# Samples' selected branch: both selections, the prompt's output norms and the half-sequence tiles moved

## The chip, the cores and the metric

The kernel runs on one core of one Trainium2 chip. The metric is the device time of one execution in microseconds (us), lower is better. Engines are named as the profile names them: PE is TensorE's matmul (PEld its weight load), DVE VectorE, ACT ScalarE, POOL GpSimd, SP SyncE, which issues most DMAs. POOL issues the gathers from the paged caches.

## What is computed

One inference step of a decoder layer for a prompt (512 tokens) and eight sample sequences (4 new tokens each on 2048 cached ones). The part that matters is the sparse attention, for prompt and samples, and what follows it:

```python
h = rmsnorm(x, w['g_mix'])
(q, kc_new, vc_new, ks_new, vs_new, kw_new, vw_new, g_nsa, xm, vm, om, i_pre, f_pre) = split_cols(h @ w['w_in'])
...
k_cmp = compress(kc_all, *w['cmp_k'])      # 16-token strides through a 2-layer net
v_cmp = compress(vc_all, *w['cmp_v'])
# nsa_attend, per block of queries:
s_c = jnp.einsum('bkgqd,bkcd->bkgqc', qi, kc) - slopes * d_c
p_c = masked_softmax(s_c, d_c >= 0)
o_c = jnp.einsum('bkgqc,bkcd->bkgqd', p_c, vc)          # compressed branch
imp = cmp_to_sel(p_c.sum(2))
...
_, idx = lax.top_k(imp, n_top)                          # selection of 64-token blocks
s_s = jnp.einsum('bkgqd,bkqsd->bkgqs', qi, k_sel) - slopes * d_s
p_s = masked_softmax(s_s, d_s >= 0)
o_s = jnp.einsum('bkgqs,bkqsd->bkgqd', p_s, v_sel)      # selected branch
...                                                     # o_w: sliding window branch
o_nsa = rmsnorm(o_nsa, w['g_head_nsa']).reshape(b, t, NSA_W)
...
mix = jnp.concatenate([o_nsa, hm.reshape(b, t, MLSTM_W).astype(x.dtype)], axis=-1) @ w['w_out']
x = x + mix
```

Cross attention, a SwiGLU layer and a final norm follow.

## The kernel before, in words

The program is written as Python generators that are woven together (`weave`, `burst`, `paced`); a scheduler then sets the order of instructions on each engine by priorities, and each engine executes its own queue in that order. Tiles come from pools with a number of buffers, so an instruction that writes a tile waits until the buffer's readers are done.

The compression of the cached values, `compress(1)`, keeps PE full with products of the split weights (`bd<-w1h,xh` and its kind, L218 to L220). A high product is made of three: the operands are split into a high and a low part by `split` (L213 on ACT makes the high part, L214 on DVE or POOL the low one). Into the compression is woven `sample()`, the samples' sparse attention. It works on two groups `g` of four sequences each. For either group its window branch comes first, then:

- the *selection*: scores against the compressed keys (`quad` with `kcT`), a softmax (tile `pcs`, Exp at L1607), block sums, a product with `GS` (L1627) and the top blocks (`t8`, `mk`), from which POOL makes the mask `M4` (L1642);
- the *key part*: keys come in half-sequence tiles `gat` (128 x 1024, 512 KB) that POOL gathers (L573). A *key turn* transposes four 128x128 blocks on PE (`four_t`, L1517) into one of two PSUM banks `tp`; `evac` copies the bank to one of four tiles `kt`, three times on ACT (L206) for one on DVE (L208). Four key turns feed one *score product* `quad` (L1527, bank `sp`), whose masked minimum DVE takes (L1653). A group has 16 key turns and 4 score products;
- the *probabilities* (`SS`, five Exps at L1674 and L1672) and the *value part*: turns of `SS` into `PTs` and 64 value products (L1693) with value tiles, which use the same `gat` buffers.

After the first group's value part stands `finals_p`, the prompt's output norm: for four pairs of heads a product with the compressed values (L1398), its addition to `oF` (L1401) and its square (ACT, L1402), a product with a matrix of ones `bones` (L1407) that leaves the mean square in a bank, then x^(-1/2) as Ln (L1408) and Exp (L1413) on ACT, and the scaling of `oF` on DVE (L1414).

Once `oF` is scaled, `early_mix` splits it (`mh`, `ml`), and the output projection's first half of tokens (272 of 544) begins: 24 products `xa/bd/xc<-mh,whi` and kin for each 128 output columns. The weights `w_out` come in four chunks of 256 columns, each of two 128x1024 pieces. The first two are fetched early (one of them into the tile `cgat`), each later one by SP (L1830, L1832) when the chunk before it in the buffer `wraw` has been split (`whi` on ACT, `wlo` on DVE). In this stretch PE uses the first two chunks, 96 products; the products of the third and fourth follow the value part of the second group.

Of the kernel before, what the change touches and what calls it, by code (L numbers as in the profile page):

```python
# [21 lines left out]
BIG = 1e30  # L22
# [14 lines left out]
def body(tc, I, O, stage=99, dbg=None):  # L37
    nc = tc.nc
    with ExitStack() as top:
# [704 lines left out]
        def need(x):  # L744
            while x not in done:
                yield 1
# [644 lines left out]
        def finals_p(var):  # L1391
            yield from need(("p", 1))
            var = var[:, :2048].rearrange("p (a b n) -> p a b n", a=2, b=2)
            for j in range(5):
# [22 lines left out]
        def sample():  # L1417
# [85 lines left out]
            def load_win(nm, b):  # L1503
                t_ = sc.tile([128, 2, 4, 128], F32, name="gat", bufs=8)
# [32 lines left out]

            win = {(0, "k"): kwin(0), (0, "v"): vwin(0), (1, "k"): kwin(1)}
            yield 2
            for g in range(2):  # L1540
                bs = [4 * g + q for q in range(4)]
# [52 lines left out]
            kg = half("cache_k_slc", 0, 0)  # L1594
            for g in range(2):
# [6 lines left out]
                quad(pc[:, 0:127], bs, lambda q: kcT[:, bs[q], 0:127])  # L1602
                pcs = sc.tile([128, 128], F32, name="pcs")
                nc.vector.memset(pcs[:, 127:128], 0.0)
                nc.vector.tensor_tensor_reduce(pcs[:, 0:127], pc[:, 0:127], K0, 1.0, BIG, op0=OP.add, op1=OP.min,
                                               accum_out=nmn[:, 0:1])
                nc.scalar.activation(pcs[:, 0:127], pcs[:, 0:127], AF.Exp, scale=-1.0, bias=nmn[:, 0:1],  # L1607
                                     accum_out=rs[:, 0:1])
                nc.vector.reciprocal(rs[:, 3:4], rs[:, 0:1])
                nc.vector.tensor_scalar(pcs[:, 0:127], pcs[:, 0:127], rs[:, 3:4], None, op0=OP.mult)  # L1610
                blk = sc.tile([128, 32], F32, name="blk")
                edge = sc.tile([128, 32], F32, name="edge")
                p4 = pcs.rearrange("p (j r) -> p j r", r=4)
                nc.vector.tensor_reduce(blk, p4[:, :, 0:3], axis=AX.X, op=OP.add)
                nc.vector.tensor_copy(edge, p4[:, :, 3])
                nc.vector.tensor_tensor(edge[:, 1:32], edge[:, 1:32], p4[:, 0:31, 3], op=OP.add)
                nc.vector.scalar_tensor_tensor(blk, edge, 0.5, blk, op0=OP.mult, op1=OP.add)
# [5 lines left out]
                p = bank(ptp)  # L1623
                nc.tensor.transpose(p[:127, :128], pcs[:, 0:127], ident)
                nc.vector.tensor_copy(pct[:127, g], p[:127, :128])
                p = bank(ptp)
                nc.tensor.matmul(p[:, :32], GSf, blk, start=True, stop=True)  # L1627
                imp = sc.tile([128, 32], F32, name="imp")
                nc.vector.tensor_copy(imp, p[:, :32])
                ia = imp[:, 1:31]  # L1630
                t8 = sc.tile([128, 16], F32, name="t8")
                nc.vector.max(out=t8[:, 0:8], in_=ia)
# [953 lines left out]
```

## Time and profile before

| what | value |
| --- | --- |
| median of 3 runs | 1249.11 us (1246.6, 1249.11, 1251.46) |
| profiled execution | 1244.16 us, of which the span is 1242.4 us |
| granted TensorE clock, mean | 0.972 |
| PE busy | 1174.2 us, 95% of the span |
| DVE, ACT, POOL busy | 67%, 50%, 45% |
| DMA | 154.30 MB, mean 124 GB/s |

The profile is of one execution, on the slowest of its cores; here there is one. Around the span lie 1.8 us of the execution's time. Busy shares are means over stages with different limits, so the stretch from 440 to 612 us, where the change works, has to be read by itself.

### The profile page before, as it was taken

The numbers are of one execution on the slowest core, as the hardware profiler recorded it, in microseconds if no ns is written. First come the engines' busy times: TensorE is split into PE (matmuls) and PEld (weight loads), VectorE is DVE, ScalarE is ACT, GpSimd is POOL, SyncE is SP. The second block draws the span as 40 slices with busy tenths as digits, with TensorE's granted clock in tenths as the row PEclk, the third lists the DMA queues.
The fourth block names the chain that finished last, engine by engine and source line by source line (L and its number), as shares of the span: only waits on it lengthen the run. The fifth ranks groups of instructions, "written<-read, shape, count | busy, mean of one in ns | idle before, by whom it ended". The sixth has DMA issues, their size and how long they took to land.

```text
span 1242.4 us, 24591 instructions
## 1 busy us (share of the span) xinstructions
PE 1174.2 (95%) x9220; PEld 1066.4 (86%) x9220; DVE 830.3 (67%) x1901; ACT 615.7 (50%) x1418; POOL 564.0 (45%) x686
## 2 busy tenths in 40 slices
PE   7999999899997989988899998999999999999996
PEld 5998999588885879846699977599899999999996
DVE  6336683567887787544566575544987887878874
ACT  5235665745646434474543233433575565565452
POOL 1013353566766366442243100034796586486442
PEclk9998999989997989998899999999999999999998
DMA  7324240141253184585468399650023322322411
GB/s 232 102 53 104 86 152 1 53 135 43 74 175 115 57 294 152 176 276 154 122 168 179 111 221 278 233 169 2 1 100 105 103 94 96 118 94 77 137 52 73
DMA packets 141769, 154.30 MB, mean 124 GB/s; under 512 B 17449, under 2 KB 123689, under 8 KB 141394
## 3 DMA queue, kind: packets, MB, share of 16 engines
q1 hardware_dynamic: 131922, 119.17, 32.1%
q0 software_dynamic: 9728, 33.56, 8.3%
q8 instruction: 73, 1.20, 0.4%
q14 instruction: 46, 0.38, 0.1%
HBM read 141.67 MB, written 13.12 MB: 125 GB/s over the span
## 4 chain that ended last, share of the span: by engine, by line
PE 53%; DVE 7%; DMA 5%; ACT 2%; issue 1%; POOL 1%; SPq 1%; POOLq 0%; DVEq 0%; ACTq 0%
PE xc L2260 7%; PE xa L2260 7%; PE bd L2260 6%; PE tp L2260 5%; PE bd L218 3%; PE bd L220 3%; PE bd L219 3%; PE xa L1296 2%; DMA wraw<-in_w_out 2%; DMA mkv<-in_cache_mem_k 2%; PE tp L1517 1%; PE bd L2159 1%; PE xc L218 1%; PE xc L219 1%; PE xc L220 1%
## 5 line engine op out<-in xcount | busy, mean ns | idle before, releaser
L214 POOL TENSOR_TENSOR al<-fraw,ah 128x512 fp32r<-128x512 f32 (+1 forms) x104 | 127.1, 1224 | 146.8 <-ACT ah L213 118.9
L213 ACT ACTIVATE whi<-wraw 128x1024 fp32r<-128x1024 f32 (+3 forms) x74 | 63.0, 890 | 70.1 <-DMA wraw<-in_w_xv 28.4
L214 DVE TENSOR_TENSOR wlo<-wraw,whi 128x1024 fp32r<-128x1024 f32 (+3 forms) x74 | 75.0, 1041 | 31.2 <-ACT whi L213 31.0
L213 ACT ACTIVATE ah<-fraw 128x512 fp32r<-128x512 f32 (+1 forms) x112 | 66.0, 594 | 43.8 <-PE xc L2260 11.8
L218 PE MATMUL bd<-w1h,xh 128*128 128x256 f32 x256 | 82.9, 326 | 0.0
L1198 POOL TENSOR_TENSOR xs<-xf 128x256 f32<-128x256 f32 x64 | 57.3, 902 | 48.5 <-PE xa L1296 29.7
L220 PE MATMUL bd<-w1h,xl 128*128 128x256 f32 x256 | 75.7, 298 | 1.4 <-DVE xl L214 1.4
L219 PE MATMUL bd<-w1l,xh 128*128 128x256 f32 x256 | 76.1, 298 | 0.0
L1296 PE MATMUL xa<-ws,xs 128*128 128x256 f32 x256 | 70.9, 399 | 1.9 <-DVE bq L1469 1.0
L625 POOL TENSOR_SCALAR sb<-sb,rs,gat 128x128 f32<-128x128 f32 (+3 forms) x64 | 46.2, 726 | 56.0 <-DVE rs L624 41.9
L213 ACT ACTIVATE xh<-xf 128x512 fp32r<-128x512 f32 x64 | 40.1, 632 | 43.6 <-DVE xf L1191 19.8
L213 ACT ACTIVATE ah<-sp 128x512 fp32r<-128x512 f32 (+1 forms) x64 | 35.6, 557 | 41.6 <-DVE sp L2200 16.9
L1191 DVE STREAM_TRANSPOSE xf<-cgat 128x512 f32<-128x512 f32 x64 | 44.9, 704 | 15.8 <-POOL xs L1198 15.0
L220 PEld LDWEIGHTS bd<-w1h,xl 128*128 128x128 f32 x256 | 49.1, 192 | 5.4 <-DVE xl L214 2.8
L219 PEld LDWEIGHTS bd<-w1l,xh 128*128 128x128 f32 x256 | 49.8, 195 | 4.3 <-issue 3.0
L214 DVE TENSOR_TENSOR xl<-xf,xh 128x512 fp32r<-128x512 f32 x64 | 48.2, 757 | 7.2 <-ACT xh L213 6.7
L1296 PEld LDWEIGHTS xa<-ws,xs 128*128 128x128 f32 x256 | 45.8, 198 | 8.1 <-issue 3.0
L218 PEld LDWEIGHTS bd<-w1h,xh 128*128 128x128 f32 x256 | 49.5, 195 | 3.7 <-issue 2.2
L219 PE MATMUL bd<-hlo,whi 128*128 128x272 f32 x176 | 52.4, 298 | 0.0
L218 PE MATMUL bd<-hhi,whi 128*128 128x272 f32 x176 | 52.2, 297 | 0.0
L220 PE MATMUL bd<-hhi,wlo 128*128 128x272 f32 x176 | 51.9, 295 | 0.0
L1874 POOL TENSOR_TENSOR acc<-acc,sq 128x272 f32<-128x272 f32 x35 | 31.4, 896 | 34.3 <-ACT sq L1873 33.9
(988 smaller groups left out, 4672.6 us busy)
## 6 DMA issues: line engine op xcount, KB each, us to landing
fraw<-in_w_gate SPq DMA_DIRECT2D x11, 1024.0 KB
fraw<-in_w_up SPq DMA_DIRECT2D x11, 1024.0 KB
fraw<-in_w_down SPq DMA_DIRECT2D x24, 384.0 KB
mkv<-in_cache_mem_k SPq DMA_DIRECT2D x64, 128.0 KB
mkv<-in_cache_mem_v SPq DMA_DIRECT2D x16, 512.0 KB
wraw<-in_w_in SPq DMA_DIRECT2D x8, 512.0 KB
wraw<-in_w_xq SPq DMA_DIRECT2D x4, 1024.0 KB
wraw<-in_w_xk SPq DMA_DIRECT2D x4, 1024.0 KB
```

Of the source, the lines that this page charges most:

```text
L213: nc.scalar.activation(hi, src, AF.Copy)
L214: (eng or nc.gpsimd).tensor_tensor(lo, src, hi, op=OP.subtract)
L218: nc.tensor.matmul(out, ah, bh, start=first, stop=False, **kw)
L219: nc.tensor.matmul(out, ah, bl, start=False, stop=False, **kw)
L220: nc.tensor.matmul(out, al, bh, start=False, stop=last, **kw)
L625: (nc.vector, nc.gpsimd)[1].tensor_scalar(sb[:, :n], sb[:, :n], rs, gat[:, i, 3 * h + 1 + br:3 * h + 2 + br], op0=OP.mult, op1=OP.mult)
L1191: nc.vector.transpose(xf.rearrange("p a (q i) -> p q a i", q=4), gs[0].rearrange("p (q t a i) -> p t q a i", q=4, t=4, a=4)[:, t])
L1198: nc.gpsimd.tensor_tensor(xs_.rearrange("p c (v j) -> p v c j", v=2), xg[:, 0], xg[:, 1], op=OP.add)
L1296: nc.tensor.matmul(dst[2], ops[2][:, kk], w1s[t][2][:, kk], start=t == 0 and kk == 0, stop=t == 3 and kk == 1, skip_group_check=True)
L1517: nc.tensor.transpose(p[:, 128 * i:128 * i + 128], srcs(i), ident)
L1874: nc.gpsimd.tensor_tensor(acc[hf], acc[hf], sq, op=OP.add)
L2260: nc.tensor.matmul(p[:, :HALF], w[a][:, k], x[b_][:, k], start=first and k == 0 and i == 0, stop=last and k == n - 1 and i == 2, skip_grou ...
```

## The change

Four things change. In `finals_p` the four Ln become four copies out of the bank, and one Ln and one Exp follow over the whole tile of 128 x 2048. The selection becomes a function `select(g)`, which runs for each group ahead of that group's window branch; the masks are kept in `sel` until the key part. `finals_p` is called ahead of the first group's key part in place of behind its value part. The tiles `gat` get ten buffers in place of eight; all four upper half-sequence key tiles of a group are asked for at once, and the second group's lower ones in two pairs, one pair sooner.

```diff
@@ finals_p
-                    nc.scalar.activation(vj, p, AF.Ln, bias=eps_t)
+                    nc.scalar.activation(vj, p, AF.Copy)
                 if j < 4:
                     yield
+            nc.scalar.activation(var, var, AF.Ln, bias=eps_t)
+            nc.scalar.activation(var, var, AF.Exp, scale=-0.5)
             for j in range(4):
                 oj, vj = oF[:, j, :512], var[:, j // 2, j % 2]
-                tc.keep_in_program_order(nc.scalar.activation(vj, vj, AF.Exp, scale=-0.5))
                 nc.vector.scalar_tensor_tensor(oj, oj, gh[:, j:j + 1], vj, op0=OP.mult, op1=OP.mult)
             yield
@@ sample: load_win and half
-                t_ = sc.tile([128, 2, 4, 128], F32, name="gat", bufs=8)
+                t_ = sc.tile([128, 2, 4, 128], F32, name="gat", bufs=10)
...
-                    t_ = cgs["free"].pop(0) if ex else sc.tile([128, 1024], F32, name="gat", bufs=8)
+                    t_ = cgs["free"].pop(0) if ex else sc.tile([128, 1024], F32, name="gat", bufs=10)
@@ sample: the selection, taken out of the loop over groups
+            sel = {}
+
+            def select(g):
+                bs = [4 * g + q for q in range(4)]
+                rs = sc.tile([128, 4], F32, name="rs4", bufs=2)
+                nmn = sc.tile([128, 12], F32, name="nmn", bufs=2)
+                yield from need(("c", 0))
+                pc = bank(psp)
+                quad(pc[:, 0:127], bs, lambda q: kcT[:, bs[q], 0:127])
+                pcs = sc.tile([128, 128], F32, name="pcs", bufs=2)
...
+                nc.vector.tensor_scalar(mk[:, 1:31], ia, -0.5 * BIG, BIG, op0=OP.is_ge, op1=OP.mult)
+                sel[g] = mk
+                yield
+
             win = {(0, "k"): kwin(0), (0, "v"): vwin(0), (1, "k"): kwin(1)}
             yield 2
             for g in range(2):
+                yield from select(g)
                 bs = [4 * g + q for q in range(4)]
@@ sample: the loop over groups of the selected branch
             kg = half("cache_k_slc", 0, 0)
+            yield from finals_p(sc.tile([128, 2080], F32, name="SS"))
             for g in range(2):
...
-                kh = half("cache_k_slc", g, 1, range(3))
-                yield from need(("c", 0))
-                pc = bank(psp)
...
+                kh = half("cache_k_slc", g, 1)
                 yield
                 kts = [keys(lambda i: kg[q][:, 128 * i:128 * i + 128]) for q in range(2)]
...
-                                            mk[:, :, None].to_broadcast([128, 32, 4]), op=OP.add)
-                kh += half("cache_k_slc", g, 1, (3,))
+                                            sel[g][:, :, None].to_broadcast([128, 32, 4]), op=OP.add)
...
+                    if c == 0 and g == 0:
+                        kg = half("cache_k_slc", 1, 0, range(2))
                     if c == 2 and g == 0:
-                        kg = half("cache_k_slc", 1, 0)
+                        kg += half("cache_k_slc", 1, 0, range(2, 4))
...
-                if g == 0:
-                    yield from finals_p(sc.tile([128, 2080], F32, name="SS"))
```

Since a scheduler sets the order on each engine, three places of the orders follow, of the kernel before and of the changed one. Lines of `sample()` are higher by 1 in the changed kernel at the key turns (L1518) and score products (L1528), and by 12 in the value part (L1705).

PE, at the end of the compression, before. `w1h` and `w1l` are the compression's weights; `gat` key tiles of the first group; L1398 is the first product of the prompt's output norm; the turns of `SS` begin the value part.

```order
L1527 MATMUL sp<-kt,Qn 32x512 x4
L1517 MATMUL tp<-ident,gat 128x128 x4
L1216 MATMUL xc<-ident,ys 128x128 x4
L218 MATMUL bd<-w1h_5412,xh 128x256
L219 MATMUL bd<-w1l_5413,xh 128x256
L220 MATMUL bd<-w1h_5412,xl 128x256
...
L1517 MATMUL tp<-ident,gat 128x128 x8
L1527 MATMUL sp<-kt,Qn 32x512 x4
L1246 MATMUL xc<-w_5309,hid 127x64 x4
L1398 MATMUL sp<-PcT,vcP 64x512 x2
L1216 MATMUL xc<-ident,ys 128x128 x4
L1517 MATMUL tp<-ident,SS 128x128 x4
```

And PE there after the change:

```order
L1407 MATMUL tp<-SS,bones 128x512
L1518 MATMUL tp<-ident,gat 128x128 x4
L1216 MATMUL xc<-ident,ys 128x128 x4
...
L220 MATMUL bd<-w1h_5412,xl 128x256
L1518 MATMUL tp<-ident,gat 128x128 x16
L1528 MATMUL sp<-kt,Qn 32x512 x4
L1518 MATMUL tp<-ident,gat 128x128 x16
L1246 MATMUL xc<-w_5309,hid 127x64 x4
L1528 MATMUL sp<-kt,Qn 32x512 x4
L1518 MATMUL tp<-ident,gat 128x128 x4
L1216 MATMUL xc<-ident,ys 128x128 x4
L1518 MATMUL tp<-ident,gat 128x128 x12
```

Before, 14 of the first group's 16 key turns and three of its four score products stand ahead of the compression's last product (L220), now one key turn and none; the eight products of the prompt's norm (L1398 and L1407) have gone the other way, the last L1407 to just ahead of that end.

ACT, at the norms, before (L1402 squares, L1408 Ln, L1607 the selection's Exp, L1413 Exp, `mh` the split of `oF`):

```order
L1402 ACTIVATE SS<-oF 128x512 x3
L1408 ACT_TABLE_LOAD
L1408 ACTIVATE SS<-tp,eps_t 128x512 x2
L1607 ACT_TABLE_LOAD
L1607 ACTIVATE pcs,rs_6684<-pcs,nmn 128x127
L1408 ACT_TABLE_LOAD
L1408 ACTIVATE SS<-tp,eps_t 128x512
L213 ACTIVATE mh<-oF 128x272 x4
L1408 ACTIVATE SS<-tp,eps_t 128x512
L1413 ACT_TABLE_LOAD
L1413 ACTIVATE SS<-SS 128x512 x3
L206 ACTIVATE kt<-tp 128x512
```

ACT there after the change (L1408 is now the copy, L1411 the Ln, L1412 the Exp, `hid` the compression's hidden layer):

```order
L1408 ACTIVATE SS<-tp 128x512
L206 ACTIVATE kt<-tp 128x512
L1411 ACT_TABLE_LOAD
L1411 ACTIVATE SS<-SS,eps_t 128x2048
L1223 ACTIVATE hid<-xc,bia 128x2x128 x2
L206 ACTIVATE kt<-tp 128x512
L1412 ACT_TABLE_LOAD
L1412 ACTIVATE SS<-SS 128x2048
L206 ACTIVATE kt<-tp 128x512
L1231 ACTIVATE hidt<-hid 128x512
```

Four table loads have become two, and the copies of the first group's key turns stand between and behind them; the copies of key turns there before were the second group's.

ACT, at the second group's key part, before; `whi<-wraw` x2 are the third and then the fourth chunk of `w_out`, the last line is the second group's probabilities:

```order
L206 ACTIVATE kt<-tp 128x512 x3
L213 ACTIVATE whi<-wraw 128x1024 x2
L206 ACTIVATE kt<-tp 128x512 x3
L213 ACTIVATE whi<-wraw 128x1024 x2
L206 ACTIVATE kt<-tp 128x512 x3
L1674 ACTIVATE SS,bs_7058<-sn,nmn 128x32
```

And there after the change; the second line is the third chunk, lines four and six the fourth:

```order
L206 ACTIVATE kt<-tp 128x512 x2
L213 ACTIVATE whi<-wraw 128x1024 x2
L206 ACTIVATE kt<-tp 128x512 x5
L213 ACTIVATE whi<-wraw 128x1024
L206 ACTIVATE kt<-tp 128x512
L213 ACTIVATE whi<-wraw 128x1024
L206 ACTIVATE kt<-tp 128x512 x4
L1686 ACTIVATE SS,bs_7091<-sn,nmn 128x32
```

Behind the third chunk's splits stand six copies of key turns before (with three of the second group's copies in the rows between the norms), ten after.

## Rows read from the trace of the kernel before

**Rows 1.** The page: the span with the number of instructions, each engine's busy time with its share of the span, and, in 40 equal slices of 31 us, PE's busy share in tenths.

```profile
span 1242.4 us, 24591 instructions
...
PE 1174.2 (95%) x9220; PEld 1066.4 (86%) x9220; DVE 830.3 (67%) x1901; ACT 615.7 (50%) x1418; POOL 564.0 (45%) x686
...
PE   7999999899997989988899998999999999999996
```

**Rows 2.** Busy time by windows, three stretches around the change: the window, its length, then busy us (and instructions) of PE, of PE's weight loads, of DVE, ACT and POOL, then the granted clock, the DMA share and GB/s.

```profile
440.00:460.00 20.00, 16.35 (x122) 14.34 (x120) 16.40 (x59) 7.11 (x14) 12.18 (x21) 0.83 0.94 324
...
460.00:528.00 68.00, 68.00 (x549) 59.15 (x551) 46.60 (x109) 30.06 (x62) 38.51 (x45) 1.00 0.53 168
...
528.00:612.00 84.00, 69.08 (x616) 46.41 (x609) 39.05 (x99) 49.50 (x99) 25.58 (x30) 0.88 0.54 175
```

**Rows 3.** Timeline of PE, the end of the compression and the products that the change moves: start us, length us, line, operation, output and inputs, shapes, count of records, and in brackets the idle time before it with its releaser.

```profile
529.04 0.60 PE L1216 MATMUL xc<-ident,ys 128*128 128x128 f32 x4
...
530.07 0.28 PE L220 MATMUL bd<-w1h,xl 128*128 128x256 f32 x1
...
530.19 1.03 PE L1517 MATMUL tp<-ident,gat 128*128 128x128 f32 x8
...
532.23 1.06 PE L1527 MATMUL sp<-kt,Qn 128*32 128x512 f32 x8 [1.00 <-ACT kt L206]
...
534.56 1.07 PE L1398 MATMUL sp<-PcT,vcP 32*64 32x512 f32 x4
...
546.65 1.12 PE L1407 MATMUL tp<-SS,bones 128*128 128x512 f32 x2
...
550.36 0.42 PE L1527 MATMUL sp<-kcT,Qn 128*32 128x127 f32 x8
```

**Rows 4.** Timeline of ACT (and, in the last line, of DVE), from the probabilities of the first selected group to the end of the prompt output's norms; columns as in the rows before.

```profile
534.84 0.31 ACT L1674 ACTIVATE SS<-sn,nmn 128x32 f32<-128x32 f32 x1
...
547.13 1.28 ACT L1408 ACT_TABLE_LOAD   x1
...
548.42 0.69 ACT L1408 ACTIVATE SS<-tp,eps_t 128x512 f32<-128x512 f32 x1
...
554.86 1.38 ACT L213 ACTIVATE mh<-oF 128x272 fp32r<-128x272 f32 x4
...
556.83 1.28 ACT L1413 ACT_TABLE_LOAD   x1
...
558.12 1.67 ACT L1413 ACTIVATE SS<-SS 128x512 f32<-128x512 f32 x3
...
559.70 0.58 ACT L206 ACTIVATE kt<-tp 128x512 f32<-128x512 f32 x1
...
558.78 2.79 DVE L1414 SCALAR_TENSOR_TENSOR oF<-oF,gh,SS 128x512 f32<-128x512 f32 x4 [2.06 <-ACT SS L1413]
```

**Rows 5.** Timeline of PE, the same norms seen from PE: the first key turns and the first score product of the second selected group, then two of the output projection's products with 23 more between them.

```profile
555.01 0.66 PE L1517 MATMUL tp<-ident,gat 128*128 128x128 f32 x4 [1.65 <-ACT SS L1408]
...
560.33 2.12 PE L1517 MATMUL tp<-ident,gat 128*128 128x128 f32 x8 [2.81 <-ACT kt L206]
...
563.74 1.93 PE L1527 MATMUL sp<-kt,Qn 128*32 128x512 f32 x6
...
572.16 0.29 PE L219 MATMUL xa<-ml,whi 128*128 128x272 f32 x1
...
575.18 0.29 PE L218 MATMUL bd<-mh,whi 128*128 128x272 f32 x1
```

**Rows 6.** Busy time by windows of 4 us, two of those behind the norms; columns as in the windows above.

```profile
556.00:560.00 4.00, 0.66 (x4) 0.42 (x4) 1.95 (x3) 3.97 (x7) 1.35 (x2) 0.71 0.55 220
...
560.00:564.00 4.00, 2.89 (x12) 1.92 (x15) 3.21 (x7) 4.00 (x10) 1.64 (x2) 0.50 0.00 0
```

**Rows 7.** Timelines of ACT, DVE and SP's DMA queue, the fetch of the third chunk of the output projection's weights (256 of its 1024 columns) and of the fourth, and their splits; the last line, of the view of the half-sequence tiles, has the time from a gather's issue to its landing.

```profile
562.93 1.05 ACT L213 ACTIVATE whi<-wraw 128x1024 fp32r<-128x1024 f32 x1
...
567.65 1.21 DVE L214 TENSOR_TENSOR wlo<-wraw,whi 128x1024 fp32r<-128x1024 f32 x1
...
568.89 1.28 SPq L1830 DMA_DIRECT2D wraw<-in_w_out  x2
...
578.28 1.06 ACT L213 ACTIVATE whi<-wraw 128x1024 fp32r<-128x1024 f32 x1 [4.91 <-DMA wraw<-in_w_out]
...
582.54 1.06 ACT L213 ACTIVATE whi<-wraw 128x1024 fp32r<-128x1024 f32 x1 [3.19 <-DMA wraw<-in_w_out]
...
584.88 1.25 SPq L1830 DMA_DIRECT2D wraw<-in_w_out  x2
...
589.62 1.06 ACT L213 ACTIVATE whi<-wraw 128x1024 fp32r<-128x1024 f32 x1 [1.30 <-DMA wraw<-in_w_out]
...
DMA to landing us min/median/max: 4.2/6.2/11.1
```

**Rows 8.** Timelines of PE and ACT, the last score products of the second group, its probabilities, and the first product after its value part.

```profile
588.91 1.07 PE L1527 MATMUL sp<-kt,Qn 128*32 128x512 f32 x8
...
594.38 1.06 PE L1527 MATMUL sp<-kt,Qn 128*32 128x512 f32 x8 [0.69 <-ACT kt L206]
...
596.67 0.32 ACT L1674 ACTIVATE SS<-sn,nmn 128x32 f32<-128x32 f32 x1 [2.34 <-DVE nmn L1668]
...
610.09 0.66 PE L1786 MATMUL sp<-ident,cgat 128*128 128x128 f32 x4
```

More of the change, by code (lines that the diff above doesn't have):

```diff
@@ L1536, in probs @@
                 return PT_
+            sel = {}
[7 more added lines that the diff above has]
+                pcs = sc.tile([128, 128], F32, name="pcs", bufs=2)
+                nc.vector.memset(pcs[:, 127:128], 0.0)
+                nc.vector.tensor_tensor_reduce(pcs[:, 0:127], pc[:, 0:127], K0, 1.0, BIG, op0=OP.add, op1=OP.min,
+                                               accum_out=nmn[:, 0:1])
+                nc.scalar.activation(pcs[:, 0:127], pcs[:, 0:127], AF.Exp, scale=-1.0, bias=nmn[:, 0:1],
+                                     accum_out=rs[:, 0:1])
+                nc.vector.reciprocal(rs[:, 3:4], rs[:, 0:1])
+                nc.vector.tensor_scalar(pcs[:, 0:127], pcs[:, 0:127], rs[:, 3:4], None, op0=OP.mult)
+                blk = sc.tile([128, 32], F32, name="blk", bufs=2)
+                edge = sc.tile([128, 32], F32, name="edge", bufs=2)
+                p4 = pcs.rearrange("p (j r) -> p j r", r=4)
+                nc.vector.tensor_reduce(blk, p4[:, :, 0:3], axis=AX.X, op=OP.add)
+                nc.vector.tensor_copy(edge, p4[:, :, 3])
+                nc.vector.tensor_tensor(edge[:, 1:32], edge[:, 1:32], p4[:, 0:31, 3], op=OP.add)
+                nc.vector.scalar_tensor_tensor(blk, edge, 0.5, blk, op0=OP.mult, op1=OP.add)
+                yield
+                p = bank(ptp)
+                nc.tensor.transpose(p[:127, :128], pcs[:, 0:127], ident)
+                nc.vector.tensor_copy(pct[:127, g], p[:127, :128])
+                p = bank(ptp)
+                nc.tensor.matmul(p[:, :32], GSf, blk, start=True, stop=True)
+                imp = sc.tile([128, 32], F32, name="imp", bufs=2)
+                nc.vector.tensor_copy(imp, p[:, :32])
+                ia = imp[:, 1:31]
+                t8 = sc.tile([128, 16], F32, name="t8", bufs=2)
+                nc.vector.max(out=t8[:, 0:8], in_=ia)
+                nc.vector.match_replace(out=ia, in_to_replace=t8[:, 0:8], in_values=ia, imm_value=-BIG)
+                nc.vector.max(out=t8[:, 8:16], in_=ia)
+                nc.vector.memset(t8[:, 13:16], -BIG)
+                nc.vector.match_replace(out=ia, in_to_replace=t8[:, 8:16], in_values=ia, imm_value=-BIG)
+                mk = sc.tile([128, 32], F32, name="mk", bufs=2)
+                nc.vector.memset(mk, 0.0)
+                nc.vector.tensor_scalar(mk[:, 1:31], ia, -0.5 * BIG, BIG, op0=OP.is_ge, op1=OP.mult)
+                sel[g] = mk
+                yield
@@ L1598, in sample @@
                 nmn = sc.tile([128, 12], F32, name="nmn", bufs=2)
-                kh = half("cache_k_slc", g, 1, range(3))
-                yield from need(("c", 0))
-                pc = bank(psp)
[L1602 to L1617, printed above, removed]
+                kh = half("cache_k_slc", g, 1)
                 yield
@@ L1622, in sample @@
                 yield
[L1623 to L1632, printed above, removed]
-                nc.vector.match_replace(out=ia, in_to_replace=t8[:, 0:8], in_values=ia, imm_value=-BIG)
-                nc.vector.max(out=t8[:, 8:16], in_=ia)
-                nc.vector.memset(t8[:, 13:16], -BIG)
-                nc.vector.match_replace(out=ia, in_to_replace=t8[:, 8:16], in_values=ia, imm_value=-BIG)
-                mk = sc.tile([128, 32], F32, name="mk")
-                nc.vector.memset(mk, 0.0)
-                nc.vector.tensor_scalar(mk[:, 1:31], ia, -0.5 * BIG, BIG, op0=OP.is_ge, op1=OP.mult)
                 M4 = sc.tile([128, 4, 128], F32, name="M4")
```

## Prediction

> **What bounds the kernel now.** I read the page first: PE is busy 95% of the span, and its 40 slices show the gaps [rows 1]. Then the windows around the samples' attention. From 460 to 528 us, while the compression runs, PE is busy 68.00 of 68.00 us at full clock: there only PE's work counts, and another engine's gain is worth nothing. From 528 to 612 PE is busy 69.08 of 84.00 us at a mean clock of 0.88 [rows 2]: 14.9 us idle, and some of the rest at half speed. This stretch the change can shorten. The timelines say what PE waits for there. The score product at 532.23 waits 1.00 us for a key tile [rows 3]. Behind the first group's value part PE stands behind ACT: 1.65 us for an Ln, then 2.81 us for a key turn's copy, which is queued behind the Exps [rows 4, 5]. The clock falls with it, to 0.71 and 0.50 [rows 6], and the second group's first score product (six of its records) takes 1.93 us, where at full clock the whole takes 1.06 [rows 3, 5]. Last, ACT waits for the third chunk of `w_out`: 4.91 us for its first piece, 3.19 for its second [rows 7], with key turns' copies queued behind. The stretch ends when the value part is done; I call 610.09 E [rows 8].
>
> **What the change moves, by stages.** The sum goes by the start of the two groups' probabilities, as both value parts and all splits hang on them: before at 534.84 and 596.67 [rows 4, 8].
>
> *Compression.* The order takes 13 key turns and three score products out of it, at 1.03/2 and 1.06 us: 9.9 us. It puts in four products L1398 (1.07 each, four records are one product) and four L1407 (two records 1.12, about 1.1 each): 8.7 us, and the second group's selection, whose product with the compressed keys takes 0.42, with its two small turns about 1 us [rows 3]. Sum -0.2, with the pipelining of what lies between 0 to +0.3; I take +0.3. The work of DVE and POOL for the selections is hidden by that full PE. One risk: two key gathers are now issued as soon as there are buffers, when DMA is at a share of 0.94 and 324 GB/s from 440 to 460, and the compression's own gathers follow [rows 2]. Two tiles of 512 KB at that rate are 3.2 us. Bounds 0 and 3.2; I take 0, since PE there is at 16.35 of 20 us and waits for more than gathers.
>
> *To the first group's probabilities.* Before, its keys were nearly all done under the compression's cover, and the probabilities came 4.5 us behind the end, 534.84 against 530.35 (530.07 + 0.28). Now one key turn is done by then. The last product with `bones` stands ahead of one key turn and 1.3 us of compression (529.04 to 530.35), so it ends at 530.35 - 1.3 - 0.5 = 528.5 [rows 3]. From there ACT's queue decides: a copy 0.6, a key tile's copy 0.5, a load 1.28, the Ln over 2048 columns, two hidden-layer activations about 0.7 (the 272-column copies are 1.38/4 each), a copy 0.5, a load 1.28, the Exp over 2048, a copy 0.5 [rows 4]. The wide operations are not in the trace: 1024 columns took 1.05 and 512 took 0.58 [rows 4, 7], so each further 512 costs 0.47 and 2048 about 2.0; the upper bound is four times 0.69. Together 9.4 us: the fourth key tile is there at 537.9, and PE has nothing to do for some 6 us of it. Score product 0 starts at 538.0. Three cycles of four key turns and a score product follow. The lower bound of a cycle is PE's own work, 2.06 + 1.06 = 3.1 us [rows 3]; the upper is 5.47, the row from 588.91 to 594.38, which holds waits for ACT [rows 8]. I take the middle, 4.3. Ahead of them DVE does the four scalings, 2.79 us [rows 4], with a key tile's copy and the first minimum queued behind, so the last score product starts at 538.0 + 12.9 + 2.8 = 553.7. From there to the probabilities took 2.29 [rows 8]; eight `mh` stand ahead of the Exps now, 2.8 us [rows 4]. I take **556.5**, 21.7 later than before; with both bounds of the cycle 552.9 to 560.0.
>
> *From there to the second group's.* Before this took 61.8 us: value part, the rest of the norms, key turns, 96 dense products. The norms are gone from it. The dense products are PE's work of 0.126 us each (24 from 572.16 to 575.18, [rows 5]), 12.1 us, now done beside the value part and the key turns. What ends last is the third chunk. The probabilities take 3.1 us (0.31 and four of 0.7); from the first split to the last low part took 5.93 (562.93 to 568.86, [rows 7]); a copy of probabilities, 0.6, now stands ahead of the fourth split, and its turn stands on PE behind 24 dense products, so up to 3 us more; I take 1.3. The chunk is then issued at 567.5, against 568.89 before: 1.4 sooner. Its second piece was split 13.65 us after issue; the fourth chunk's first piece came in 4.74 where the third's took 9.39 [rows 7]. Gathers land in 4.2 to 11.1 us, so they share the queue's rate [rows 7]; before, the second group's value gathers were in flight with the third chunk, and the new order has as many there. I take 13.65: 581.2. Behind it on ACT and DVE are its split 1.06, low part 1.22 and a key tile's copy 0.69, so score product 0 starts at 584.1; three cycles of 4.3 and 2.29 give the probabilities at **599.3**, 2.6 later than before. Ten copies of key turns stand on ACT behind that chunk where six stood; that is where the 1.4 us goes and more.
>
> *From there to E* 13.4 us, as before: the same value part, and its tiles come no later.
>
> A rule of the Trainium skill bears on the loads. Before, four loads lay here, the first at 547.13, the last at 556.83, each 1.28 us, with the next activation right behind it (547.13 + 1.28, then 548.42) [rows 4]; two are left, so 2.6 us of ACT are saved, all within the stretch that the sum above replaces. The Trainium skill, "ScalarE: Activation LUTs", section "What ACT_TABLE_LOAD costs", puts a switch at about 1.28 us plus a drain of 1.38. The trace has no drain behind the load. By the page the two loads left on the path would cost 2.8 us more than I count, and the sum would be 5.7, still within half a percent.
>
> **Sum.** +0.3 + 2.6 = +2.9 us on the profiled execution of 1244.16, 1247.1. The median of the runs shown is 1249.11, 5 us above that execution, so I forecast 1252. Half a percent, 6.2 us, is about what a measurement of this kernel can tell from no change.
>
> **Rivals.** *Faster: the chunk no longer gates.* If the gathers are out of the way, the third chunk comes as the fourth did, 9.39 - 4.74 = 4.65 us sooner, and the key turns, with the norms gone from their midst, go at PE's pace of 3.1 us: six cycles, -7.2. That gives 2.9 - 11.8 = -8.9, 1240. For it: the stalls of 1.65 and 2.81 at the norms, and half-clock work, are gone from the second group. Against: the chunk's issue hardly moves, and ACT, which copies three of four key tiles, is the busiest engine next to PE in this stretch, 49.50 us [rows 2]. It decides from cycles below 3.6 us together with the quick chunk. *Slower: the first group's keys without cover.* A key part that PE did beside full-rate work now runs by itself; PE waits for copies, the clock sits at 0.50 as it does from 560 to 564 [rows 6], and cycles run at 5.47. Six cycles cost 7.0 us more: +9.9, 1259. It alone decides from a cycle of 4.9 us on. *The gathers ahead of the compression's* add their 3.2: +6.1, 1255, just inside no change.
>
> **How the numbers follow.** My forecast, including its neighbours within 6.2 us, has 0.48; the slower rival, alone or with a part of the gathers, 0.31; the faster rival 0.21. The range from 1242 to 1262 takes in the slower rival with 3 us of the gathers and most of what lies on the way to the faster one, leaving out its far end and the mishaps beyond. So faster 0.21, same 0.48, slower 0.31.
>
> **What would show it.** Right: in the changed profile the compression ends at 530 to 531 with PE full; two table loads behind it; then a window with PE mostly idle and a clock near 0.5 around 532 to 540, which did not exist; the first group's probabilities near 556; a wait of ACT for the third chunk near 570 to 581; no stall of PE behind Ln or Exp later; E near 613. Wrong: the probabilities of the first group before 552, a third chunk that lands within 6 us of its issue, or score products less than 3.6 us apart, would make it faster; a compression that ends past 533, or score products 5 us apart and more, slower.

## The result and the profile after

Median 1261.4 us after (12 runs, 1254.16 to 1266.54) against 1247.4 before (12 runs beside them, 1243.16 to 1253.51): ratio 1.0106, 95% interval 1.0084 to 1.0129. The changed kernel is slower by 1.1%, 13.2 us by this ratio (the medians lie 14.0 apart). That is inside the range of the prediction, by 0.6 us; the case held likeliest, no change, did not come, and the time is close to the slower rival's 1259.

The page of the changed kernel, the span, the engines' busy time, then PE's busy share and granted clock in 40 slices:

```profile
span 1260.7 us, 24597 instructions
...
PE 1182.6 (94%) x9220; PEld 1072.6 (85%) x9220; DVE 840.5 (67%) x1901; ACT 612.3 (49%) x1414; POOL 558.7 (44%) x686
...
PE   7999999899996989968899998999999999999996
...
PEclk9998999899997999977899999999999999999998
```

The span is 18.3 us longer than in [rows 1]. Not all of it is the change: up to 440 us the orders on all engines are the same, and yet an issue of SP there (the ninth `nxt<-cur`) stands at 419.12 where it stood at 415.53. So 3.6 us lies between two executions of the same work; 14.9 us came behind it, up to E.

The windows of [rows 2] after; columns as there:

```profile
440.00:460.00 20.00, 15.54 (x127) 13.64 (x127) 18.05 (x68) 6.36 (x16) 14.02 (x23) 0.91 1.02 347
460.00:528.00 68.00, 65.82 (x499) 55.10 (x499) 47.63 (x123) 30.97 (x65) 37.07 (x43) 1.00 0.50 159
528.00:612.00 84.00, 66.24 (x491) 47.52 (x489) 33.45 (x57) 40.09 (x69) 23.65 (x28) 0.84 0.58 189
```

These windows are fixed in time, and the changed kernel is late in them. The same work, from the compression's end to E, before and then after:

```profile
530.35:610.09 79.74, 64.82 (x579) 42.70 (x576) 35.63 (x89) 46.32 (x91) 22.45 (x27) 0.87 0.54 178
536.62:628.59 91.97, 71.36 (x620) 50.62 (x618) 38.06 (x80) 43.97 (x82) 24.23 (x29) 0.81 0.51 167
```

ACT does 2.4 us less there than before and DVE 2.4 us more. PE has 41 more instructions, is idle 20.6 us for 14.9, and its clock is 0.81 for 0.87. ACT's work shrank; PE's waits grew.

The two stages of the prediction, as windows: end of the compression to the first group's probabilities (A), and from these to the second group's (B). Before:

```profile
530.35:534.84 4.49, 3.22 (x27) 1.95 (x26) 3.34 (x9) 2.48 (x6) 1.95 (x3) 1.00 1.00 282
534.84:596.67 61.83, 49.85 (x394) 32.32 (x390) 28.19 (x62) 36.18 (x65) 19.15 (x22) 0.89 0.62 208
```

After:

```profile
536.62:569.40 32.78, 19.66 (x113) 12.19 (x110) 16.13 (x30) 18.52 (x32) 12.42 (x16) 0.75 0.58 193
569.40:615.65 46.25, 40.08 (x347) 29.54 (x347) 17.93 (x31) 18.94 (x32) 11.23 (x12) 0.88 0.60 195
```

A grew by 28.3 us, B shrank by 15.6. In A PE is now idle 13.1 of 32.8 us, at a clock of 0.75. What it waits for stands on ACT's timeline (with the first row, of PE, the compression's last product):

```profile
536.34 0.28 PE L220 MATMUL bd<-w1h,xl 128*128 128x256 f32 x1
...
536.18 1.28 ACT L1411 ACT_TABLE_LOAD   x1
537.47 2.00 ACT L1411 ACTIVATE SS<-SS,eps_t 128x2048 f32<-128x2048 f32 x1
...
540.71 1.28 ACT L1412 ACT_TABLE_LOAD   x1
542.00 1.91 ACT L1412 ACTIVATE SS<-SS 128x2048 f32<-128x2048 f32 x1
543.82 0.58 ACT L206 ACTIVATE kt<-tp 128x512 f32<-128x512 f32 x1
...
569.40 0.32 ACT L1686 ACTIVATE SS<-sn,nmn 128x32 f32<-128x32 f32 x1 [3.57 <-DVE nmn L1680]
...
572.74 1.04 ACT L213 ACTIVATE whi<-wraw 128x1024 fp32r<-128x1024 f32 x1
...
594.00 2.01 ACT L213 ACTIVATE whi<-wraw 128x1024 fp32r<-128x1024 f32 x2 [2.94 <-PE bd L219]
```

And on PE's, a key turn that waits behind the Ln, the first group's four score products, the turns of its probabilities, the first dense product of `w_out`, the second group's first score product and E:

```profile
540.74 0.66 PE L1518 MATMUL tp<-ident,gat 128*128 128x128 f32 x4 [2.02 <-ACT kt L206]
544.45 1.93 PE L1528 MATMUL sp<-kt,Qn 128*32 128x512 f32 x8 [3.05 <-ACT kt L206]
...
548.11 2.91 PE L1518 MATMUL tp<-ident,gat 128*128 128x128 f32 x12 [0.69 <-ACT kt L206]
...
552.55 1.94 PE L1528 MATMUL sp<-kt,Qn 128*32 128x512 f32 x8
...
558.36 1.06 PE L1528 MATMUL sp<-kt,Qn 128*32 128x512 f32 x8
...
563.35 1.06 PE L1528 MATMUL sp<-kt,Qn 128*32 128x512 f32 x8
570.76 1.97 PE L1518 MATMUL tp<-ident,SS 128*128 128x128 f32 x8 [6.34 <-ACT SS L1684]
...
574.58 0.57 PE L218 MATMUL xa<-mh,whi 128*128 128x272 f32 x1
...
600.75 1.07 PE L1528 MATMUL sp<-kt,Qn 128*32 128x512 f32 x8
...
628.59 0.66 PE L1798 MATMUL sp<-ident,cgat 128*128 128x128 f32 x4
```

Ln and Exp end 7.3 us behind the compression (543.91 against 536.62), and PE waits 2.02 and 3.05 us for copies queued behind them. Windows of 4 us show what that does to the clock, which sits at 0.50, the lower of its two levels (1.2 GHz), from 544 to 556 and again from 568 to 576, each time behind a stretch in which PE did 0.66 and 0.42 us of work:

```profile
540.00:544.00 4.00, 0.66 (x4) 0.42 (x4) 0.06 (x1) 3.97 (x5) 0.95 (x1) 0.82 0.94 339
...
552.00:556.00 4.00, 4.00 (x19) 2.22 (x20) 1.30 (x3) 0.64 (x2) 0.00 (x0) 0.50 0.64 235
...
564.00:568.00 4.00, 0.42 (x4) 0.00 (x0) 3.61 (x4) 1.84 (x6) 3.98 (x9) 0.80 0.84 293
...
572.00:576.00 4.00, 4.00 (x43) 3.20 (x42) 3.28 (x7) 4.00 (x8) 0.00 (x0) 0.50 0.00 0
```

The second hole, 6.34 us, lies between the last score product and the probabilities. Timelines of DVE and POOL there:

```profile
565.10 3.77 DVE L214 TENSOR_TENSOR ml<-oF,mh 128x272 fp32r<-128x272 f32 x1
...
564.20 1.49 POOL L214 TENSOR_TENSOR ml<-oF,mh 128x272 fp32r<-128x272 f32 x2
565.64 1.50 POOL L1655 TENSOR_TENSOR M<-B,mk 128x128 f32<-128x128 f32 x4
567.11 1.46 POOL L214 TENSOR_TENSOR ml<-oF,mh 128x272 fp32r<-128x272 f32 x2
```

DVE's low part of `oF` takes 3.77 us where the ones behind it take 0.43, and ends when POOL's run of eight operations does; the steps to the probabilities are queued behind it.

### The profile page after: what moved, and what is told of

It reads as the page before. It is cut to its first block, busy times and chain, and to the rows that moved or that the text cites. A ratio compares the mean times of both kernels' runs of the same rounds, so it can differ in the third digit from the quotient of the medians.

```text
span 1260.7 us, 24597 instructions
## 1 busy us (share of the span) xinstructions
PE 1182.6 (94%) x9220; PEld 1072.6 (85%) x9220; DVE 840.5 (67%) x1901; ACT 612.3 (49%) x1414; POOL 558.7 (44%) x686
## 4 chain that ended last, share of the span: by engine, by line
PE 49%; DVE 8%; DMA 3%; ACT 2%; issue 2%; SPq 1%; POOL 1%; POOLq 0%; DVEq 0%; ACTq 0%
PE xa L2272 7%; PE xc L2272 7%; PE bd L2272 5%; PE tp L2272 5%; PE bd L219 3%; PE bd L218 3%; PE bd L220 3%; PE tp L1518 2%; DMA mkv<-in_cache_mem_k 2%; PE xa L218 1%; PE bd L2171 1%; PE xa L219 1%; PE xa L220 1%; PE xc L218 1%; PE xc L219 1%
## 5 line engine op out<-in xcount | busy, mean ns | idle before, releaser
L220 PE MATMUL bd<-w1h,xl 128*128 128x256 f32 x256 | 75.4, 297 | 3.1 <-DVE xl L214 3.1
L1198 POOL TENSOR_TENSOR xs<-xf 128x256 f32<-128x256 f32 x64 | 54.9, 864 | 52.5 <-PE xa L1296 28.3
L213 ACT ACTIVATE xh<-xf 128x512 fp32r<-128x512 f32 x64 | 40.1, 629 | 48.1 <-DVE xf L1191 29.6
L220 PEld LDWEIGHTS bd<-w1h,xl 128*128 128x128 f32 x256 | 48.9, 192 | 6.4 <-DVE xl L214 3.9
L1191 DVE STREAM_TRANSPOSE xf<-cgat 128x512 f32<-128x512 f32 x64 | 44.4, 700 | 13.1 <-POOL xs L1198 11.1
L218 PE MATMUL bd<-hhi,whi 128*128 128x272 f32 x176 | 51.9, 295 | 0.0
L214 DVE TENSOR_TENSOR xl<-xf,xh 128x512 fp32r<-128x512 f32 x64 | 46.8, 735 | 7.3 <-ACT xh L213 5.0
L220 PE MATMUL bd<-hhi,wlo 128*128 128x272 f32 x176 | 51.5, 293 | 0.0
L214 DVE TENSOR_TENSOR al<-sp,ah 128x512 fp32r<-128x512 f32 (+1 forms) x64 | 40.7, 636 | 10.3 <-ACT ah L213 8.6
```

The lines of the kernel that those rows point to most:

```text
L213: nc.scalar.activation(hi, src, AF.Copy)
L214: (eng or nc.gpsimd).tensor_tensor(lo, src, hi, op=OP.subtract)
L218: nc.tensor.matmul(out, ah, bh, start=first, stop=False, **kw)
L220: nc.tensor.matmul(out, al, bh, start=False, stop=last, **kw)
L1191: nc.vector.transpose(xf.rearrange("p a (q i) -> p q a i", q=4), gs[0].rearrange("p (q t a i) -> p t q a i", q=4, t=4, a=4)[:, t])
L1198: nc.gpsimd.tensor_tensor(xs_.rearrange("p c (v j) -> p v c j", v=2), xg[:, 0], xg[:, 1], op=OP.add)
```

## The experiments

The change has four parts: the move of `finals_p` (*move*), `select(g)` ahead of the window branch (*select*), ten tiles with their gathers (*tiles*), one Ln and Exp (*one Ln*). Theories for the loss: **U**, every key turn that loses the compression's cover costs about alike; **N**, the norms' Ln and Exp, where they now stand, hold up ACT and so the first group's keys; **D**, ten tiles put gathers ahead of transfers that PE needs; **I**, move and select cost only together.

All kernels in one table: the ratio to the kernel before, with its interval; the stages from each kernel's profile (compression from the issue of `nxt<-cur` named above to the last L220, A, B, and C to E); PE's idle time in all four plus what half clock took from its work, by windows of 1 us; and the end of the norms' last Ln or Exp against that of the compression. PE's work at full clock in the stages is 160.6 to 167.7 us in all of them, while idle time and clock go from 23.6 to 42.0: times differ mainly by these. The stages are of one execution each, which can lie off the kernel's median: e7's is 4.4 us faster, e6's 4.1 and e3's 1.8 us slower.

| kernel | ratio | compr. | A | B | C | idle + clock | Exp's end |
|---|---|---|---|---|---|---|---|
| before | 1 | 114.8 | 4.5 | 61.8 | 13.4 | 29.5 | behind, by design |
| after | 1.0106 [1.0084, 1.0129] | 117.5 | 32.8 | 46.2 | 12.9 | 41.8 | 7.3 behind |
| e1 | 0.9980 [0.9957, 1.0003] | 114.7 | 4.5 | 60.4 | 11.3 | 27.1 | behind, by design |
| e2 | 0.9969 [0.9948, 0.9989] | 118.4 | 18.3 | 47.8 | 11.3 | 29.9 | 13.0 ahead |
| e3 | 1.0025 [1.0000, 1.0050] | 110.1 | 16.8 | 59.2 | 13.5 | 38.6 | behind, by design |
| e4 | 1.0023 [0.9996, 1.0051] | 113.5 | 4.2 | 67.8 | 13.5 | 34.9 | behind, by design |
| e5 | 1.0032 [1.0007, 1.0058] | 107.6 | 15.2 | 57.2 | 15.2 | 32.1 | behind, by design |
| e6 | 1.0026 [0.9999, 1.0052] | 116.2 | 17.8 | 51.9 | 15.3 | 36.7 | 9.9 ahead |
| e7 | 1.0068 [1.0038, 1.0097] | 116.2 | 24.6 | 46.8 | 10.6 | 33.1 | 2.1 behind |
| e8 | 1.0073 [1.0040, 1.0107] | 113.7 | 26.1 | 49.4 | 10.6 | 36.1 | 3.1 behind |
| e9 | 0.9964 [0.9941, 0.9987] | 119.4 | 24.4 | 39.5 | 10.6 | 27.8 | 1.6 ahead |
| e10 | 1.0110 [1.0074, 1.0145] | 115.8 | 35.1 | 45.4 | 12.2 | 42.0 | 7.3 behind |
| e11 | 0.9975 [0.9946, 1.0005] | 115.5 | 24.9 | 36.1 | 12.4 | 23.6 | none |
| e12 | 1.0043 [1.0017, 1.0068] | 121.2 | 13.7 | 50.2 | 13.4 | 31.5 | 14.0 ahead |

**Each part alone, on the kernel before.** e1, one Ln:

```diff
-                    nc.scalar.activation(vj, p, AF.Ln, bias=eps_t)
+                    nc.scalar.activation(vj, p, AF.Copy)
...
+            nc.scalar.activation(var, var, AF.Ln, bias=eps_t)
+            nc.scalar.activation(var, var, AF.Exp, scale=-0.5)
...
-                tc.keep_in_program_order(nc.scalar.activation(vj, vj, AF.Exp, scale=-0.5))
```

> Before with the norms' edit alone: four copies, one Ln and one Exp over 2048 columns; place of the norms, selections and tiles as before. On PE 14 of the first group's 16 key turns and three of its four score products stay ahead of the compression's end, as before. Theory U (what costs time is the first group's key turns that lose the compression's cover, about 1 us each: 13 turns, some 13 us): no turn moves, so 0, with 2.6 us of table loads less on ACT, -3 to +1 us. Rival N (the wide Ln and Exp, 9 us in a row ahead of key turns' copies, are the cost): +4 us or more, since they now stand in one block ahead of the second group's key turns. Rival D (the gathers issued earlier are the cost): 0.

e2, the move alone:

```diff
             kg = half("cache_k_slc", 0, 0)
+            yield from finals_p(sc.tile([128, 2080], F32, name="SS"))
...
-                if g == 0:
-                    yield from finals_p(sc.tile([128, 2080], F32, name="SS"))
```

> Before with finals_p called ahead of the first group's key part, with its four Ln and four Exp as they were; selections and tiles as before. On PE 7 of the 16 key turns and one score product stay ahead of the compression's end, where 14 and three did. Theory U: 7 turns lose their cover, +5 to +9 us. Rival N: +10 us or more, as four Ln and Exp with loads between them stand ahead of the key turns. Rival D: 0.

e3, select alone:

```diff
             for g in range(2):
+                yield from select(g)
                 bs = [4 * g + q for q in range(4)]
...
```

> Before with both selections ahead of the window branches, norms and tiles as before. On PE 8 of the 16 key turns and one score product stay ahead of the compression's end; the second window score product stands 91 compression products ahead of the end where it stood 156. Theory U: 6 turns lose their cover, +4 to +8 us. Rival N: 0, as the norms stay behind the first group's value part. Rival D: 0.

e4, tiles alone:

```diff
-                t_ = sc.tile([128, 2, 4, 128], F32, name="gat", bufs=8)
+                t_ = sc.tile([128, 2, 4, 128], F32, name="gat", bufs=10)
...
-                kh = half("cache_k_slc", g, 1, range(3))
+                kh = half("cache_k_slc", g, 1)
...
-                        kg = half("cache_k_slc", 1, 0)
+                        kg += half("cache_k_slc", 1, 0, range(2, 4))
```

> Before with ten half-sequence tiles and the gathers' new order alone. On PE 14 of the 16 key turns and three score products stay ahead of the compression's end. Theory U: -2 to +2 us. Rival N: 0. Rival D: +4 us or more, and a transfer nxt<-cur of some 10 us in the compression's second block, as in the changed kernel (11.57 us in its chain).

The four give -0.20, -0.31, +0.25 and +0.23%, together nothing (each is known to about 0.25); the change gives +1.06%. So the loss is in how the parts meet. The move by itself shows no loss though it leaves 9 of the first group's 16 key turns behind the compression (2 before): A grows by 13.8 us and B shrinks by 14.0. U would have made that cost; it is weakened. The tiles alone cost at most 0.5%, so D is at most a part; the transfer of some 10 us that was to show it is not in e4's chain, where the one `nxt<-cur` takes 4.56 us.

**The change without one part.** e5 leaves out the move, e6 select (its call goes back to the group's key part), e7 the tiles, e8 has four Ln and Exp again:

```diff
@@ e5, against the changed kernel
-            yield from finals_p(sc.tile([128, 2080], F32, name="SS"))
...
+                if g == 0:
+                    yield from finals_p(sc.tile([128, 2080], F32, name="SS"))
@@ e6
-                yield from select(g)
...
                 kh = half("cache_k_slc", g, 1)
+                yield from select(g)
@@ e7
-                t_ = sc.tile([128, 2, 4, 128], F32, name="gat", bufs=10)
+                t_ = sc.tile([128, 2, 4, 128], F32, name="gat", bufs=8)
...
@@ e8
-                    nc.scalar.activation(vj, p, AF.Copy)
+                    nc.scalar.activation(vj, p, AF.Ln, bias=eps_t)
...
```

> The changed kernel with finals_p back behind the first group's value part (still one Ln and one Exp; selections ahead, ten tiles). On PE 6 of the 16 key turns and one score product are ahead of the compression's end, against one and none in the changed kernel. Theory U (about 1 us for each key turn without cover): 10 turns without cover where before had 2: +8 us against before, -5 against the changed kernel. Rival N (the norms ahead of the keys are the whole cost): 0 against before. Rival D (the gathers' order): +13, as the changed kernel.

> The changed kernel with each selection back at the head of its group's key part. On PE 5 of the 16 key turns and no score product are ahead of the compression's end. Theory U: 11 turns without cover, +9 us against before. Rival N: +13, as the changed kernel, as the norms still stand ahead of the keys. Rival D: +13.

> The changed kernel with eight half-sequence tiles and the gathers' old order. On PE 3 of the 16 key turns and no score product are ahead of the compression's end. Theory U: +11 us against before. Rival D: 0 to +4 against before, and no long nxt<-cur transfer. Rival N: +13.

> The changed kernel with the four Ln and four Exp of before, in the new place. On PE one of the 16 key turns is ahead of the compression's end, as in the changed kernel. Theory U: +13 us against before, as the changed kernel, 0 to 3 more for the table loads. Rival N (one block of 9 us in a row is the cost): less than the changed kernel by 4 or more.

Leaving out move or select gives back most of it (1.0032, 1.0026), tiles or one Ln a third (1.0068, 1.0073), which the intervals barely tell from nothing. That fits I, and N as well: in e7, e8 and after, the last Exp ends 2.1, 3.1 and 7.3 us behind the compression, in e6 9.9 ahead of it. Four Ln in place of one don't cure it: in e8 PE's hole ahead of the probabilities' turns is there as in after.

```profile
555.46 1.97 PE L1517 MATMUL tp<-ident,SS 128*128 128x128 f32 x8 [6.33 <-ACT SS L1683]
...
559.27 0.57 PE L218 MATMUL xa<-mh,whi 128*128 128x272 f32 x1
```

**e9, move and select together**, with four Ln and eight tiles (the edits of e2 and e3):

```diff
             for g in range(2):
+                yield from select(g)
...
+            yield from finals_p(sc.tile([128, 2080], F32, name="SS"))
             for g in range(2):
...
```

> Before with two edits: finals_p ahead of the first key part and both selections ahead; eight tiles, four Ln and four Exp. On PE 3 of the 16 key turns and no score product stay ahead of the compression's end. Singly the norms ahead gave a ratio of 0.997 and the selections ahead 1.0025. Theory I (the two edits work on one thing: either leaves about half of the first group's keys under the compression, together they leave none, and the rest runs behind the norms with PE idle and at half clock): ratio 1.006 or more, 20 us or more from the compression's end to the first group's probabilities. Rival S (the edits' costs add up, and tiles or the one Ln make up the changed kernel's loss): ratio 0.997 to 1.002.

0.9964, faster than before: I falls, and S, by which the two edits' costs add up, is met within the interval. U falls too: 13 key turns and all score products stand behind the compression's end, and A is 24.4 us, yet nothing is lost. PE, ACT, DVE and (last row) POOL in e9:

```profile
535.22 1.06 PE L1527 MATMUL sp<-kt,Qn 128*32 128x512 f32 x8 [0.52 <-ACT kt L206]
...
550.05 1.06 PE L1527 MATMUL sp<-kt,Qn 128*32 128x512 f32 x8 [2.50 <-ACT kt L206]
551.04 0.47 PE L218 MATMUL xa<-mh,whi 128*128 128x272 f32 x1
...
531.62 0.62 ACT L1413 ACTIVATE SS<-SS 128x512 f32<-128x512 f32 x1
...
549.88 1.06 ACT L213 ACTIVATE whi<-wraw 128x1024 fp32r<-128x1024 f32 x1
...
558.18 0.32 ACT L1686 ACTIVATE SS<-sn,nmn 128x32 f32<-128x32 f32 x1 [4.41 <-DVE nmn L1680]
...
554.09 2.57 DVE L214 TENSOR_TENSOR wlo<-cgat,whi 128x1024 fp32r<-128x1024 f32 x2
...
556.87 1.21 DVE L214 TENSOR_TENSOR wlo<-wraw,whi 128x1024 fp32r<-128x1024 f32 x1
...
554.24 4.49 POOL L1654 TENSOR_TENSOR M<-B,mk 128x128 f32<-128x128 f32 x4 [1.78 <-DVE nmn L1665]
```

The last Exp ends at 532.2, ahead of the compression's end at 533.82, and the first score product comes 1.4 us behind that end, not 7.8. The probabilities take 8.1 us from the last score product, longer than in after (6.05), but PE has work: the `whi` splits stand on ACT ahead of the probabilities, so dense products begin at 551.04, directly behind the score product. In after, e7 and e8 the splits stand behind the probabilities: the stretch takes 6.05, 6.04 and 6.05 us, with PE busy for 1.07 of it.

**e10, all low parts of `oF` on POOL**, to take DVE's 3.77 us away:

```diff
-                split(hot[0][0][:, k], hot[0][1][:, k], oF[:, k, :HALF], nc.gpsimd if k % 2 else nc.vector)
+                split(hot[0][0][:, k], hot[0][1][:, k], oF[:, k, :HALF], nc.gpsimd)
```

> The changed kernel with all eight low parts ml of early_mix on POOL in place of four on POOL and four on DVE. In the changed kernel DVE's chain to the first group's probabilities stands behind four ml, one of which took 3.77 us while POOL made masks and low parts, 0.43 the others. Theory: the probabilities start 3 us or more sooner behind the last score product (6.05 us there, near 2.3 to 2.9 now), the time -3 us, or less if the first dense products then wait for the low parts. Rival: the last masks or ACT's eight mh set the start, and nothing changes.

No gain (1.0110): the wait moved to the next DVE operation of that kind. Timelines of DVE and POOL:

```profile
561.17 6.23 DVE L1678 TENSOR_TENSOR nmn<-nmn,slc 128x4 f32<-128x4 f32 x1
...
560.14 2.90 POOL L214 TENSOR_TENSOR ml<-oF,mh 128x272 fp32r<-128x272 f32 x4
563.01 1.50 POOL L1655 TENSOR_TENSOR M<-B,mk 128x128 f32<-128x128 f32 x4
564.48 2.89 POOL L214 TENSOR_TENSOR ml<-oF,mh 128x272 fp32r<-128x272 f32 x4
```

**e11, the changed kernel without Ln and Exp**, which leaves x^(-1/2) of the prompt's norm out:

```diff
-            nc.scalar.activation(var, var, AF.Ln, bias=eps_t)
-            nc.scalar.activation(var, var, AF.Exp, scale=-0.5)
```

> The changed kernel with the Ln and the Exp of the prompt's output norm left out: the scaling multiplies by the mean square itself. It measures what the two wide operations and their table loads cost where they stand. In the changed kernel the first group's first score product starts 7.8 us behind the compression's end, and PE is idle 13.0 us and loses 5.5 us to a half clock from there to the probabilities. If the block of loads, Ln and Exp is what PE waits for: first score product within 3 us of the end, time -6 to -10 us. If the key turns' own pace is the cost: first score product 5 us sooner, but the probabilities less than 4 us sooner, time -1 to -4 us.

0.9975 against 1.0106: the 6.5 us of two loads, one Ln and one Exp take 1.3%, 16 us, of the time, more than the 6 to 10 expected. The same stages, in e11:

```profile
534.01:558.90 24.89, 20.57 (x149) 14.16 (x147) 16.96 (x32) 16.29 (x32) 15.72 (x14) 0.93 0.73 257
558.90:594.97 36.07, 30.02 (x313) 20.85 (x311) 13.06 (x27) 15.48 (x29) 12.69 (x15) 1.00 0.72 248
```

The clock is 0.93 and 1.00 for 0.75 and 0.88. B falls with A because the order turned as in e9: dense products begin at 553.61, ahead of the probabilities at 558.90. So the 16 us is the block *and* the order that the scheduler chose around it; this run does not split the two.

**e12, move and one Ln**, on the kernel before (the edits of e1 and e2):

```diff
-                    nc.scalar.activation(vj, p, AF.Ln, bias=eps_t)
+                    nc.scalar.activation(vj, p, AF.Copy)
...
+            yield from finals_p(sc.tile([128, 2080], F32, name="SS"))
             for g in range(2):
...
```

> Before with the two edits that were each not slower alone: finals_p ahead of the first key part, with one Ln and one Exp; selections inside their group, eight tiles. On PE 8 of the 16 key turns and one score product stay ahead of the compression's end, and the norms end about 71 compression products ahead of it, so the wide Ln and Exp lie under full PE. Theory I: the gains of the two add, ratio 0.993 to 0.997 against before. Rival N (the one block of Ln and Exp ahead of key turns costs wherever it stands): ratio above 1.000.

1.0043 against e2's 0.9969: early, one Ln costs 9 us more than four, although its Exp ends 14 us ahead of the compression's end. The gains of e1 and e2 do not add, as I would have it; the ratio is above 1, as N would. Its compression is 2.8 us longer, and dense products begin at 560.32 for 555.39. Why is not settled.

**What follows.** By parts: every kernel more than half a percent slower than before (e7, e8, after, e10) has move and select with tiles or one Ln or both. Move and select alone (e9) beat both kernels: 0.36% faster than before. From e9, tiles alone (e8) cost 1.1 points and one Ln alone (e7) 1.0; both (after) 1.4.

As its expectations had it, N did not hold: it put e1 at +4 us or more, e2 at +10 or more and e6 at +13, and they came at 0.9980, 0.9969 and 1.0026. A narrower reading, made after those runs, fits: with the move, kernels whose last Exp ends ahead of the compression lie at 0.9964 to 1.0043, those where it ends behind at 1.0068 to 1.0110, the slowest where it ends last (e7 and e8 can't be told apart, and hardly from after). The first dense product, counted from the compression's end, divides them alike: 17.2 us in e9, 19.6, 22.7, 23.8 and 24.9 in e11, e6, e2 and e12, then 29.7, 31.2, 38.0 and 40.1 in e7, e8, after and e10.

This is supported, not shown, since no run moves the Exp's end and keeps the order. A rival stands beside it: the second hole, which is the same 6 us in e7, e8 and after, whatever the first one was, and which dense products fill in e9 and e11. No run changes that order alone. Open too are the price of one Ln when it is early (e12), and how much of the 1.1 points between e9 and e8 is the gathers and how much the order that comes with them.

## Why the prediction was right and wrong

Its sum was +2.9 on the profiled execution; the stages measure +2.7 + 28.3 - 15.6 - 0.5 = +14.9. That the range held is in part luck: 1261.4 lies 0.6 us inside its end, and on the 1249.11 that the forecast went by, the measured ratio gives 1262.3. The forecast itself, 1252, was wrong, and two of the terms below are why.

- *Compression, +0.3.* Measured +2.7. PE has 2.2 us idle from 460 to 528 where it had none [rows 2]. The gathers' risk was priced at 3.2, but kernels with ten tiles have 107.6 to 117.5, so no steady cost of theirs shows. Of the 2.7, 1.7 does not come with the order: e10, whose orders on all engines are the same up to the low parts of `oF`, takes 115.8, +1.0. In the changed kernel's profile the chain has a transfer `nxt<-cur` of 11.57 us from 456.96, and PE waits 1.4 us for the copy behind it; in e10 it waits nothing there.
- *To the first group's probabilities, 26.2.* Measured 32.8. ACT's queue was right: first score product 7.83 us behind the compression's end for 7.65, Ln and Exp 2.00 and 1.91 for 2.0, and a load with the next activation right behind it (536.18 + 1.28, then 537.47), as in [rows 4]. The Trainium skill, "ScalarE: Activation LUTs", section "What ACT_TABLE_LOAD costs", adds a drain of 1.38 us; these rows don't show it. What failed is the next term, three cycles of 4.3 with DVE's 2.8, 15.7 in all: measured 18.9, as 8.1, 5.81 and 4.99. The hole was foreseen and its price was not: behind it score products take 1.93 us and not 1.06. I took a middle of rows at full clock, though [rows 5, 6] showed half clock behind a smaller stall. From the first of these score products to the last took 14.8 us in e9 and e11, at a clock of 1.00 and 0.99, and 18.9 here at 0.69: 15.7 would have done without the hole. The last term failed too: 2.8 to the probabilities, measured 6.05, by DVE's stall beside POOL, with nothing else ready for PE.
- *To the second group's, 42.8.* Measured 46.2. The cause named was wrong. The chunk was issued 9.27 us behind the probabilities (11.0 predicted), and its splits at 594.00 were released by a product of PE, not by the DMA. What ended last was PE's own queue: value part and 96 dense products, which cannot begin before 574.58 and run partly at half clock, so the second group's score product 0 came 31.35 us behind the probabilities for 27.6. Its three cycles took 12.6 (12.9) and the rest 2.28 (2.29): the cycle of 4.3 was right where the clock was.
- *To E, 13.4.* Measured 12.9.
- *The rivals.* The slower one came, 1.1% for its 0.8%, by its half clock, but in the first group alone: two of its three cycles there were longer than 5.47 (the sign for slower was 5 and more), the second group's were not slow, and keys without cover don't cost by themselves (e2, e9). The faster one named the wrong lever: the gathers and the chunk did not decide. Its pace of 3.1 a cycle shows in no group, even without Ln and Exp: e11's cycles are 4.8, 4.2 and 5.9, then 5.4, 3.8 and 3.7.

## What to carry to other kernels

A block on an in-order engine is priced by what PE can do while it runs: four Ln and Exp cost nothing where they end before the work that keeps PE full does (e2, e9), and the one block, with the order that came of it, took 16 us for its 6.5 where it ends behind (e11 against after), since PE pays for the hole again in half clock. An early place is no warrant: one Ln there was 9 us dearer than four (e12), and why is open. Before moving work out of a full stretch, look for the dense products that could fill the new holes, and at whether their operands' splits stand ahead of or behind the wait in the queue. Parts that are harmless alone can lose together, so a change of several parts is best tried with each left out.

## What the runs showed of the hardware

Two DVE operations of two operands stood still while POOL worked: 3.77 us for a split that takes 0.43, and in e10 6.23 us for 128 x 4 elements, each ending within 0.3 us of the end of POOL's whole row of operations, back to back. The Trainium skill, "SBUF — State Buffer", section "Who interferes with whom", says that a DVE instruction with two SBUF inputs contends with a GpSimd instruction that reads SBUF. The trace agrees, and here the wait was for several in a row (564.20 to 568.57, and 560.14 to 567.37). It goes the other way too: in e9 POOL's four mask operations took 4.49 us beside DVE's `wlo`, 1.50 in after.
